# Strassen steps in more of a decoder layer's products

## The chip, the core and the metric

The kernel runs on one core of one Trainium2 chip. The metric is device time of one execution in microseconds (us), as the median of several runs. TensorE (PE) multiplies, VectorE (DVE) and ScalarE (ACT) do elementwise work, GpSimd (POOL) little here, SyncE (SP) issues the loads of the weights.

## The reference, cut to what matters

One layer of a decoder for 256 tokens with a model width of 2048, all in float32.

```
h  = RMSNorm(x);  z = h @ W_in          # W_in: 2048 x 19472
q, k, v, g, lr = first columns of z     # gated linear attention: 1024, 1024, 2048, 2048, 16
gk = log_sigmoid(lr @ w_gk_up + b_gk) / 16
A  = GLA(q, k, v, gk) * silu(g), normed # 4 heads, keys 256, values 512 wide
Bm = dilated attention on 9 x 1024 columns of z
y  = sigmoid(ga) * (A @ W_a) + sigmoid(gb) * (Bm @ W_b)
x  = x + y @ W_out                      # 2048 x 2048
x  = x + (silu(n @ W_gate) * (n @ W_up)) @ W_down,  n = RMSNorm(x)   # width 5632
out = RMSNorm(x)
```

## The kernel before, in words

Every product is a Job. Its weights stream in units of 1 MB at most through a ring of three raw tiles (dma). Each unit is cut into pieces of at most 1024 columns of float32 (subs). ACT rounds a piece to fp32r (wh), DVE subtracts to get the rest (wl), and TensorE forms a product as three matmuls: high by high, high by low, low by high. The activations are split the same way beforehand (HiLo).

Jobs have kinds. "T" holds the activations as stationary operand and moves the weights (512 columns in two PSUM banks); "F" holds the weights and moves 256 tokens; "G" is F with high and low activations in one matmul. "S" takes two column blocks of 512 at once in eight steps of 256 weight rows (add_steps, lines 161 to 190); a step listed in `fast` forms seven block products instead of eight, with sums of weight blocks made by DVE (sums, L187) and sums of activation blocks made beforehand (x1_forms, L886 to 900). An S job needs all eight PSUM banks: of p2, p3, p4, p8 and of p1, p5, p6, p7 one set lies in the four acc banks, the other in psa and psb, and `turn` says which (step_bank, L218).

The order is written out. The main loop goes through all pieces; for piece i it splits piece i + 4 (LA = 4; the wh and wl rings have five buffers each, and from the feed-forward S jobs on there is a sixth pair in z8 and z9), then, at the first piece of a job, evacuates the job before (pending.evac), runs a hook (pre), advances the queue of side work by one, issues the piece's matmuls, and advances the queue by one again. Side work are generators in a first-in first-out queue: attention heads, transposes (turn_block, ffn_norm_chunk), the forms. `drain` runs what is left of a tag at once. Each engine works through its own instructions in the order in which they were issued.

Only ten feed-forward jobs (fast_pair) are S jobs, each with three fast steps (2, 4, 6). The linear attention's values, gates, keys and queries, the output projection (w_out, four T jobs) and the down products (down: groups of 4, 4 and 3 blocks of 512 rows, four T jobs each) are plain. The 16 columns of the decay input lr ride behind the gates of heads 2 and 3: 1040 columns are cut into three T jobs of 348, 346 and 346 columns, which run first.

Of the kernel before, what the change touches and what calls it, by code (L numbers as in the profile page):

```python
# [23 lines left out]
NEG = -1e30  # L24

# [21 lines left out]
class Job:  # L47
# [14 lines left out]
    def __init__(self, kind, w, row0, nkt, col0, ncols, ktu, acts, evac, pre=None, pairs=None,  # L62
                 col1=None, fast=(), forms=None, turn=0):
        self.pairs = pairs
        self.col1, self.fast, self.forms = col1, fast, forms
        self.bank, self.turn = {}, turn
# [6 lines left out]
def trunk_layer(ctx: ExitStack, tc: tile.TileContext, x, attn_norm, w_in, w_gk_up, b_gk, gla_norm,  # L73
# [114 lines left out]
    def sums(sub):  # L188

        if sub.get("src") not in ("t13", "t24"):  # L190
            return
        b = raw_step(sub["unit"])
        if sub["src"] == "t13":
            t = sub["unit"]["t"] = env["fp"].tile([P, 4, 512], F32, name="t", tag="t")
            nc.vector.tensor_sub(t[:, 0:2], b[:, :, 1], b[:, 0])
        else:
            t = sub["unit"]["t"]
            nc.vector.tensor_sub(t[:, 2], b[:, 1, 1], t[:, 0])
            nc.vector.tensor_sub(t[:, 3], b[:, 1, 0], t[:, 2])  # L199

    def step_src(sub):
        b = raw_step(sub["unit"])
        src = sub["src"]
        if src == "b11":
            return b[:, 0, 0:1]
        if src[0] == "b":
            return b[:, int(src[1]) - 1]
        return sub["unit"]["t"][:, 0:2] if src == "t13" else sub["unit"]["t"][:, 2:4]
# [90 lines left out]
    def mains(sub, only=None, part=None):  # L299
# [6 lines left out]
        if not hasattr(job, "acc"):  # L306
# [6 lines left out]
            elif n <= 256:  # L313
                t = ps_acc()
                job.acc = [t[:, 0:256], t[:, 256:512]]
# [137 lines left out]
    def view(key, slot, a, fresh=True):  # L453

        if key not in env:
            env[key] = block("z", slot).rearrange("p (a t) -> p a t", a=a)
# [15 lines left out]
    def g_chunk(lo, hi, slots, base):  # L472

        def go(job):
            for a in range(2):
                c = lo
                while c < hi:
                    sc = env["rstd"][:, a:a + 1]
                    if c >= 1024:
                        act(lrn[:, a], job.acc[a][:, c - lo:hi - lo], AF.Copy, scale=sc)  # L480
                        c = hi
                        continue
                    j = c // 512
                    e = min(hi, (j + 1) * 512)
                    g = view(("g", base + j), slots[j], 2)
                    act(g[:, a, c - j * 512:e - j * 512], job.acc[a][:, c - lo:e - lo],
                                         AF.Silu, scale=sc)
                    c = e
        return go
# [10 lines left out]
    def evac_zf(key, slot):  # L500
        def go(job):
            scaled(job, view(key, slot, 4), "R")
        return go
# [11 lines left out]
    def gla_head(h, half):  # L515
# [94 lines left out]
        hl = hl_block("o", {2: 4, 3: 6, 0: 0, 1: 2}[h])  # L610
# [25 lines left out]
    def open_dil():  # L636
        drain("bias")
        drain("B")
# [94 lines left out]
    def win(kind, col, n, evac, pre=None):  # L733
        add(Job(kind, w_in, 0, KT, col, n, 8 if n <= 256 else 4, h_acts, evac, pre))

    def start_half(tag, heads):
        def go():
            for h in heads:
                push(tag, gla_head(h, tag))
        return go  # L740

    c0 = C_G + 1024
    for lo, hi in ((0, 348), (348, 694), (694, 1040)):
        ev = g_chunk(lo, hi, (0, 1), 2)
        if hi == 1040:
            def ev(job, f=ev):
                f(job)
                push("A", gla_lr())
        win("T", c0 + lo, hi - lo, ev)
    win("F", C_K + 512, 512, evac_zf(("k", "A"), 2))  # L750
    win("F", C_Q + 512, 512, evac_zf(("q", "A"), 3))
    win("T", C_V + 1024, 512, evac_t(("v", 2), 4))
    win("T", C_V + 1536, 512, evac_t(("v", 3), 5, start_half("A", (2, 3))))
    win("T", C_G, 512, g_chunk(0, 512, (6, 7), 0))
    win("T", C_G + 512, 512, g_chunk(512, 1024, (6, 7), 0))
    win("F", C_K, 512, evac_zf(("k", "B"), 8))
    win("F", C_Q, 512, evac_zf(("q", "B"), 9), {0: lambda: drain("A")})
    win("T", C_V, 512, evac_t(("v", 0), 0))

    def after_b():  # L760
        start_half("B", (0, 1))()
        push("bias", bias_table())
    win("T", C_V + 512, 512, evac_t(("v", 1), 1, after_b))


# [8 lines left out]
    for r in range(4):  # L774
        for g in range(3):
            base = C_DIL + 3072 * g + 256 * r
            first = {0: lambda r=r: drain(f"D{r - 2}")} if g == 0 else None
            slot = ((2, 3, 4), (8, 0, 1))[r % 2][g]
# [7 lines left out]
        if r % 2 == 0:  # L786

            for g in range(3):
                then = (first_heads if r == 0 else lambda: push_heads(2)) if g == 2 else None
                first = {0: lambda r=r: drain("D1" if r else "B")} if g == 1 else None  # L790
# [92 lines left out]
    FAST = (2, 4, 6)  # L883
    x1F = {}

    def x1_forms():  # L886

        yield from idle(1)
        for n, st in enumerate(FAST):
            t = x1T[st // 2].t[st % 2]  # L890
            a = env["fp"].tile([P, 2, S], F32, name="fa", tag="u0")
            f = env["fp"].tile([P, 4, P], F32, name="ff", tag="u1")
            nc.vector.tensor_add(a, t[:, :, 0].bitcast(F32), t[:, :, 1].bitcast(F32))
            nc.vector.tensor_add(f[:, 0], a[:, 0, P:], a[:, 1, P:])
            nc.vector.tensor_sub(f[:, 2], a[:, 0, 0:P], a[:, 0, P:])
            nc.vector.tensor_sub(f[:, 1], f[:, 0], a[:, 0, 0:P])
            nc.vector.tensor_sub(f[:, 3], a[:, 1, 0:P], f[:, 1])
            b = x1F[st] = block("o", n, F32R).rearrange("p (w f q) -> p w f q", w=2, f=4)
            act(b[:, 0], f, AF.Copy)
            nc.vector.tensor_sub(b[:, 1], f, b[:, 0].bitcast(F32))  # L900
            yield
            yield

    def ffn_norm_chunk(c):
# [5 lines left out]
        if c == 3:  # L910
# [3 lines left out]
            push("F", x1_forms())  # L914

    def evac_out(c):
        def go(job):
            for a in range(2):
                nc.vector.tensor_add(x1[c][:, a], job.acc[a], x1[c][:, a])
                junk = env["fp"].tile([P, 512], F32, name="junk", tag="u3")  # L920
                act(junk, x1[c][:, a], AF.Square, accum_out=ss1[:, a, c:c + 1])
# [18 lines left out]

    def turn_up(p, z, n, pair):
        aT[p] = hl_block("z", 2 * p % 8)
        push("A", turn_block(z, aT[p], n, pair))

# [9 lines left out]
    def evac_step1(job):  # L954

        u = job.u = [env["fp"].tile([P, 512], F32, name=f"u{i}", tag=f"u{i}") for i in range(4)]
        b = job.bank
        act(u[0], b["p1"], AF.Copy)
        nc.vector.tensor_add(u[1], u[0], b["p6"])
        nc.vector.tensor_add(u[2], u[1], b["p7"])  # L960
        nc.vector.tensor_add(u[1], u[1], b["p5"])
        nc.vector.tensor_add(u[3], u[2], b["p5"])

    def evac_step2(p):
        def go(job):
            u, b = job.u, job.bank
            z = env["fp"].tile([P, 2, 512], F32, name="sg", tag="sg", bufs=2)
            nc.vector.tensor_add(z[:, 0], u[0], b["p2"])
            act(z[:, 0], z[:, 0], AF.Silu, scale=env["rstd2"][:, 0:1])
            nc.vector.tensor_add(u[1], u[1], b["p3"])  # L970
            nc.vector.tensor_add(z[:, 1], u[2], b["p4"])
            act(z[:, 1], z[:, 1], AF.Silu, scale=env["rstd2"][:, 1:2])
            nc.vector.tensor_add(u[3], u[3], b["p8"])
            for a in range(2):
                nc.vector.scalar_tensor_tensor(z[:, a], u[1 + 2 * a], env["rstd2"][:, a:a + 1], z[:, a],
                                               op0=ALU.mult, op1=ALU.mult)
            turn_up(p, z, 2, 2 * job.turn)
        return go

    def evac_down(c, last):  # L980
        def go(job):
            for a in range(2):
                nc.vector.tensor_add(x1[c][:, a], job.acc[a], x1[c][:, a])
                if last:
                    junk = env["fp"].tile([P, 512], F32, name="junk", tag="u3")
# [13 lines left out]
    def fast_pair(p, turn):  # L999
        def start():  # L1000
            drain("F")
            drain("A")
        job = Job("S", w_ffn_in, 0, KT, 512 * p, 512, 2, x1_acts, evac_step2(p), {4: start}, None,
                  FF + 512 * p, FAST, lambda st: x1F[st], turn)
        add(job)
        job.pre[len(job.subs) - 2] = lambda: evac_step1(job)

    def down(p0, n, last):
        acts = lambda ki, p0=p0: (aT[p0 + ki // 4], ki % 4)
        for c in range(4):  # L1010
            pre = {2 * (n - 1): lambda: drain("A")} if c == 0 else None
            if c == 0 and last:
                pre[0] = load_fg
            add(Job("T", w_ffn_out, p0 * 512, 4 * n, 512 * c, 512, 4, acts, evac_down(c, last), pre,
                    pairs=[((3, 0, 1, 3), (0, 1, 0, 3))[p0 == 4][c]]))

    pair(0)
    for p in range(1, 11):
        fast_pair(p, (0, 0, 1, 0, 0, 1, 0, 1, 0, 1, 0)[p])
# [13 lines left out]
    more = next(i for i, s in enumerate(subs) if s["job"].kind == "S") + LA + 1  # L1033
# [47 lines left out]
    def input_rstd():  # L1081
# [5 lines left out]
        env["R"] = row_bcast("R", env["rstd"])  # L1087

# [38 lines left out]
    def add_tokens(src, a, q):  # L1127
        w = slice(q * S, q * S + S)
        nc.vector.tensor_add(x1[3][:, a, w], src, x1[3][:, a, w])
        junk = env["fp"].tile([P, 512], F32, name="junk", tag="u3")  # L1130
# [74 lines left out]
```

## Time and profile before

| | us |
|---|---|
| median of 3 runs (1863.65 to 1865.05) | 1864.06 |
| the profiled execution | 1863.59 |
| its span, first to last instruction | 1861.5 |
| TensorE busy in the span | 1847.5 |
| VectorE busy | 1197.6 |
| ScalarE busy | 913.2 |

The profile is one execution. The page gives busy time by engine, 40 slices of the span and groups of instructions; the chain of waits follows the work that ended last, backwards from the end. The timeline shows instructions in order with the time that the engine stood idle before them and what released it. Matmuls are pipelined: the length shown for one contains its way through the array, so the distance between starts is what one costs.

### The profile page before, as it was taken

The numbers are of one execution on the slowest core, as the hardware profiler recorded it, in microseconds if no ns is written. First come the engines' busy times: TensorE is split into PE (matmuls) and PEld (weight loads), VectorE is DVE, ScalarE is ACT, GpSimd is POOL, SyncE is SP. The second block draws the span as 40 slices with busy tenths as digits, with TensorE's granted clock in tenths as the row PEclk, the third lists the DMA queues.
The fourth block names the chain that finished last, engine by engine and source line by source line (L and its number), as shares of the span: only waits on it lengthen the run. The fifth ranks groups of instructions, "written<-read, shape, count | busy, mean of one in ns | idle before, by whom it ended". The sixth has DMA issues, their size and how long they took to land.

```text
span 1861.5 us, 23268 instructions
## 1 busy us (share of the span) xinstructions
PE 1847.5 (99%) x9234; PEld 1572.2 (84%) x9234; DVE 1197.6 (64%) x1394; ACT 913.2 (49%) x1144; POOL 22.3 (1%) x35
## 2 busy tenths in 40 slices
PE   8999999999999999999999999999999999999998
PEld 8988988888888888888888888888888888888887
DVE  6446646745665466655545556789647998559974
ACT  6446545544444444544444455555435555335553
POOL 0000000000000000000000000000000000000001
PEclk9999999999999999999999999999999999999999
DMA  7554455455555566466656655555655655545562
GB/s 253 205 195 167 159 187 176 162 182 186 179 176 181 192 182 209 147 199 207 205 201 218 234 182 180 192 193 204 219 188 189 217 183 205 201 161 203 202 236 103
DMA packets 208580, 356.33 MB, mean 191 GB/s; under 512 B 7403, under 2 KB 67879, under 8 KB 208472
## 3 DMA queue, kind: packets, MB, share of 16 engines
q1 hardware_dynamic: 203472, 346.19, 54.1%
q0 software_dynamic: 1728, 5.51, 1.4%
q10 hardware_dynamic: 3272, 3.16, 0.6%
q8 instruction: 72, 1.18, 0.2%
q14 instruction: 36, 0.29, 0.0%
HBM read 352.70 MB, written 2.13 MB: 191 GB/s over the span
## 4 chain that ended last, share of the span: by engine, by line
PE 99%; DMA 0%; DVE 0%; ACT 0%; SPq 0%; issue 0%; DVEq 0%; ACTq 0%
PE acc L356 51%; PE acc L236 12%; PE acc L332 10%; PE psb L356 6%; PE psa L236 5%; PE acc L335 5%; PE psb L236 5%; PE psa L672 1%; PE psb L717 0%; PE psa L593 0%; PE psa L818 0%; PE psb L575 0%; PE psb L682 0%; PE psb L719 0%; PE acc L818 0%; PE psa L693 0%
## 5 line engine op out<-in xcount | busy, mean ns | idle before, releaser
L133 ACT ACTIVATE wh<-raw 128x1024 fp32r<-128x1024 f32 (+3 forms) x614 | 625.8, 1026 | 633.6 <-PE acc L356 435.6
L296 DVE TENSOR_TENSOR wl<-raw,wh 128x1024 fp32r<-128x1024 f32 (+2 forms) x482 | 580.9, 1212 | 505.7 <-ACT wh L133 503.8
L356 PE MATMUL acc<-wh,h 128*128 128x512 f32 (+2 forms) x1536 | 469.8, 383 | 0.0
L356 PEld LDWEIGHTS acc<-wh,h 128*128 128x128 f32 x1536 | 286.6, 188 | 54.2 <-issue 1.3
L356 PE MATMUL acc<-wl,h 128*128 128x512 f32 (+2 forms) x768 | 292.9, 381 | 0.0
L332 PE MATMUL acc<-h,wh 128*128 128x512 f32 x768 | 196.4, 397 | 0.0
L356 PE MATMUL acc<-wh,z 128*128 128x512 f32 x600 | 187.8, 390 | 0.0
L289 DVE TENSOR_TENSOR wl<-raw,wh 128x1024 fp32r<-128x1024 f32 (+1 forms) x132 | 143.1, 1100 | 42.3 <-ACT wh L133 41.9
L356 PEld LDWEIGHTS acc<-wl,h 128*128 128x128 f32 x768 | 144.7, 188 | 25.5
L332 PEld LDWEIGHTS acc<-h,wh 128*128 128x128 f32 x768 | 138.5, 189 | 26.9 <-issue 0.7
L236 PE MATMUL acc<-wh,h 128*128 128x512 f32 x446 | 146.7, 390 | 0.0
L356 PEld LDWEIGHTS acc<-wh,z 128*128 128x128 f32 x600 | 112.6, 188 | 23.2
L356 PE MATMUL acc<-wl,z 128*128 128x512 f32 x300 | 116.7, 389 | 0.0
L335 PEld LDWEIGHTS acc<-h,wl 128*128 128x128 f32 x768 | 104.6, 190 | 7.8
L335 PE MATMUL acc<-h,wl 128*128 128x256 f32 x768 | 106.9, 282 | 0.0
L236 PEld LDWEIGHTS acc<-wh,h 128*128 128x128 f32 x446 | 83.7, 188 | 17.3
L356 PE MATMUL acc<-h,wh 128*128 128x256 f32 x512 | 92.5, 283 | 0.0
L236 PE MATMUL acc<-wl,h 128*128 128x512 f32 x223 | 86.8, 389 | 0.0
L133 ACT ACTIVATE wh<-t 128x1024 fp32r<-128x1024 f32 x51 | 54.1, 1060 | 58.4 <-DVE t L199 26.5
L356 PEld LDWEIGHTS acc<-h,wh 128*128 128x128 f32 x512 | 80.0, 192 | 0.2
L356 PE MATMUL acc<-wh,o 128*128 128x512 f32 x256 | 79.4, 389 | 0.0
L356 PE MATMUL psb<-wh,z 128*128 128x512 f32 (+1 forms) x248 | 75.8, 381 | 0.0
(276 smaller groups left out, 2308.6 us busy)
## 6 DMA issues: line engine op xcount, KB each, us to landing
raw<-in_w_in_dram SPq DMA_DIRECT2D x144, 1024.0 KB, 4.7
raw<-in_w_ffn_in_dram SPq DMA_DIRECT2D x160, 512.0 KB, 4.4
raw<-in_w_ffn_out_dram SPq DMA_DIRECT2D x44, 1024.0 KB, 5.0
raw<-in_w_branch_gla_dram SPq DMA_DIRECT2D x16, 1024.0 KB, 5.0
raw<-in_w_out_dram SPq DMA_DIRECT2D x16, 1024.0 KB, 4.9
raw<-in_w_branch_dil_dram SPq DMA_DIRECT2D x8, 1024.0 KB, 4.9
raw<-in_w_ffn_in_dram SPq DMA_DIRECT2D x8, 1024.0 KB, 4.7
raw<-in_w_in_dram SPq DMA_DIRECT2D x8, 692.0 KB, 4.0
```

The costliest lines, as they stand in the source:

```text
L133: nc.scalar.activation(o, i, func, **kw)
L236: nc.tensor.matmul(job.bank[pr["b"]], st, mv, start=pr["first"] and i == 0, stop=pr["last"] and i == 2, skip_group_check=True)
L289: nc.vector.tensor_sub(wl, src, wh.bitcast(F32))
L296: nc.vector.tensor_sub(wl[:, :k * n], src, wh[:, :k * n].bitcast(F32))
L332: nc.tensor.matmul(job.acc[j], wh[:, kk, c], hl.both(aj), start=ki == 0, stop=ki == job.nkt - 1, skip_group_check=True)
L335: nc.tensor.matmul(job.acc[j][:, 0:S], wl[:, kk, c], hl.hi(aj), start=False, stop=ki == job.nkt - 1, skip_group_check=True)
L356: nc.tensor.matmul(dst, st, mv, start=first and i == 0 and j % per_bank == 0, stop=last and i == 2, skip_group_check=True)
L672: nc.tensor.matmul(p1[:, g * 256:(g + 1) * 256], qk[g][:, 0, 128:256], qk[g][:, 1], start=g != 1, stop=True, skip_group_check=True)
```

## The change: what it does

The S job is put into one function (fast_job) with its two evacuations, and used in more places. The forms of the activations (act_forms) are made for the normed input, for the merged heads, and for parts of the feed-forward activations.

- Gates and values of the linear attention: four S jobs with three fast steps each, on heads (2, 3) and (0, 1). The keys and queries of heads 2 and 3 come first, then lr as a T job of its own with 16 columns, in one unit of 16 blocks of 128 rows, then the four S jobs, then keys and queries of heads 0 and 1. Heads 2 and 3 are pushed behind the last S job.
- Output projection: chunk 0 as a T job, chunks 1 and 2 as one S job with three fast steps, chunk 3 as a T job in the psb banks.
- Down product: in the first two groups two S jobs with two fast steps (2, 5) each; the third stays.
- The sums of weight blocks have two tiles (t13, t24) instead of one. The `turn` of the feed-forward jobs follows a new list, and the banks of the last down jobs as well.

```diff
+    def act_forms(blocks, out, dst, tmp, steps=FAST):
+        yield from idle(1)
+        for n, st in enumerate(steps):
+            t = blocks[st // 2].t[st % 2]
+            a, f = tmp(0).rearrange("p (a q) -> p a q", a=2), tmp(1).rearrange("p (f q) -> p f q", f=4)
+            nc.vector.tensor_add(a, t[:, :, 0].bitcast(F32), t[:, :, 1].bitcast(F32))
+            nc.vector.tensor_add(f[:, 0], a[:, 0, P:], a[:, 1, P:])
...
+            act(b[:, 0], f, AF.Copy)
+            nc.vector.tensor_sub(b[:, 1], f, b[:, 0].bitcast(F32))
+            yield
+            yield
+
+    def fast_job(w, col0, col1, acts, forms, turn, tile, dst, evac, pre, row0=0, fast=FAST, plus=None):
+        def first(job):
+            c = job.c = dst()
+            b = job.bank
+            act(c[0], b["p1"], AF.Copy)
+            nc.vector.tensor_add(c[1], c[0], b["p6"])
+            nc.vector.tensor_add(c[2], c[1], b["p7"])
+            nc.vector.tensor_add(c[1], c[1], b["p5"])
+            nc.vector.tensor_add(c[3], c[2], b["p5"])
+            if plus:
+                job.u, job.c = c, plus()
+                for u, c in zip(job.u, job.c):
+                    nc.vector.tensor_add(c, c, u)
+        def second(job):
+            for i, n in ((0, "p2"), (2, "p4"), (1, "p3"), (3, "p8")):
+                nc.vector.tensor_add(job.c[i], job.c[i], job.bank[n])
+                evac(job, i)
+        job = Job("S", w, row0, KT, col0, 512, 2, acts, second, pre, None, col1, fast, lambda st: forms[st], turn, tile)
+        add(job)
+        job.pre[next(i for i, s in enumerate(job.subs) if s["step"] > max(fast))] = lambda: first(job)
...
+    def evac_lr(job):
+        for a in range(2):
+            act(lrn[:, a], job.acc[a], AF.Copy, scale=env["rstd"][:, a:a + 1])
+        push("L", gla_lr())
...
-    for lo, hi in ((0, 348), (348, 694), (694, 1040)):
...
-        win("T", c0 + lo, hi - lo, ev)
...
-    win("T", C_V + 512, 512, evac_t(("v", 1), 1, after_b))
+    win("F", C_K + 512, 512, evac_zf(("k", "A"), 6))
+    win("F", C_Q + 512, 512, evac_zf(("q", "A"), 7))
+    win("T", C_LR, 16, evac_lr)
+    win_fast("g", (2, 3), (3, 5), C_G + 1024, 0, AF.Silu, {4: first_fast})
+    win_fast("g", (0, 1), (8, 9), C_G, 1, AF.Silu, {})
+    win_fast("v", (2, 3), (2, 4), C_V + 1024, 0, AF.Copy, {})
+    win_fast("v", (0, 1), (0, 1), C_V, 1, AF.Copy, {}, last_values)
+    win("F", C_K, 512, evac_zf(("k", "B"), ("o", 0)))
+    win("F", C_Q, 512, evac_zf(("q", "B"), ("o", 1), after_b))
...
-    for c in range(4):
-        add(Job("T", w_out, 0, KT, 512 * c, 512, 4, merged_acts, evac_out(c),
-                {0: reload_x} if c == 0 else None))
+    def out_forms():
+        reload_x()
+        push("mF", act_forms(merged, mF, lambda n: fp_forms(n) if n < 2 else block("o", 2, F32R),
+                             lambda i: block("o", i)[:, 0:512]))
...
+    add(Job("T", w_out, 0, KT, 0, 512, 4, merged_acts, evac_out(0), {0: out_forms}))
+    fast_job(w_out, 512, 1024, merged_acts, mF, 0, fp_tile, four_halves, evac_out2, {4: out_start},
+             plus=lambda: four_x1(1))
+    add(Job("T", w_out, 0, KT, 1536, 512, 4, merged_acts, evac_out(3), pairs=[3]))
...
     def turn_up(p, z, n, pair):
         aT[p] = hl_block("z", 2 * p % 8)
         push("A", turn_block(z, aT[p], n, pair))
+        if p in (1, 2, 5, 6):
+            st, f = ((2, 0), (5, 1))[p % 4 - 1]
+            push("A", act_forms([None] * (st // 2) + [aT[p]], aF, lambda n: fp_forms(f),
+                                lambda i: fp_half(f"u{i}"), (st,)))
...
     def down(p0, n, last):
+        if not last:
+            for c in (0, 2):
+                turn = int(c == 0)
+                pre = {4: lambda: drain("A")} if c == 0 else {}
+                fast_job(w_ffn_out, 512 * c, 512 * c + 512, acts, aF, turn, fp_tile, four_halves,
+                         lambda job, i: None, pre, p0 * 512, (2, 5), lambda c=c: four_x1(c))
+            return
```

## Rows read from the trace of the kernel before

**Rows 1.** The page: busy time of each engine, and VectorE's tenths in 40 slices.

```profile
PE 1847.5 (99%) x9234; PEld 1572.2 (84%) x9234; DVE 1197.6 (64%) x1394; ACT 913.2 (49%) x1144; POOL 22.3 (1%) x35
...
DVE  6446646745665466655545556789647998559974
```

**Rows 2.** The chain of waits in order of time: start us, length us, what.

```profile
1166.70 21.76 PE psb L356 x96
...
1848.60 4.33 PE psa L356 x36
```

**Rows 3.** Two stretches: length; busy us of PE, PEld, DVE, ACT, POOL; clock, DMA share, GB/s.

```profile
33.00:57.00 24.00, 24.00 (x153) 24.00 (x153) 12.47 (x13) 14.00 (x21) 0.00 (x0) 1.00 0.67 226
...
1244.00:1286.40 42.40, 42.40 (x192) 35.17 (x191) 38.80 (x44) 24.23 (x28) 0.00 (x0) 1.00 0.58 198
```

**Rows 4.** Timeline of TensorE, 1238 to 1282: start us, length us, engine, line.

```profile
1238.84 1.03 PE L818 MATMUL acc<-ident,sg 128*128 128x128 f32 x8
...
1273.05 0.39 PE L236 MATMUL acc<-wh,h 128*128 128x512 f32 x1
...
1281.21 1.03 PE L818 MATMUL psa<-ident,sg 128*128 128x128 f32 x8
```

**Rows 5.** Timeline of TensorE and its weight loads (PEld), 162 to 165.

```profile
162.48 1.06 PE L575 MATMUL psb<-qe,ke 128*128 128x128 f32 x8
...
163.38 0.61 PE L575 MATMUL psb<-mA,sA 128*128 128x128 f32 x4
...
163.91 0.54 PEld L575 LDWEIGHTS psb<-qe,kd 128*64 128x64 f32 x8
...
164.52 0.19 PEld L356 LDWEIGHTS acc<-wh,h 128*128 128x128 f32 x1
...
164.63 0.19 PEld L356 LDWEIGHTS acc<-wl,h 128*128 128x128 f32 x1
```

**Rows 6.** Stretches at the program's start and end, columns as in rows 3.

```profile
4.00:8.00 4.00, 2.38 (x10) 1.78 (x10) 1.84 (x4) 1.55 (x4) 0.00 (x0) 1.00 1.03 340
...
1850.00:1853.00 3.00, 2.92 (x25) 2.71 (x23) 0.04 (x1) 0.00 (x0) 0.00 (x0) 1.00 0.52 193
...
1856.00:1857.00 1.00, 0.00 (x0) 0.00 (x0) 0.99 (x2) 0.23 (x1) 0.00 (x0) 0.77 0.19 76
```

**Rows 7.** Groups of instructions by shape: busy us, mean ns, idle before.

```profile
L133 ACT ACTIVATE wh<-raw 128x1024 fp32r<-128x1024 f32 x560 | 589.7, 1058 | 611.1 <-PE acc L356 429.0 <-PE acc L332 71.8 <-PE psb L356 36.3
...
L296 DVE TENSOR_TENSOR wl<-raw,wh 128x1024 fp32r<-128x1024 f32 x458 | 560.1, 1229 | 495.1 <-ACT wh L133 493.3
```

**Rows 8.** Timeline of all engines, 0 to 40.

```profile
6.11 0.78 ACT L133 ACTIVATE wh<-raw 128x696 fp32r<-128x696 f32 x1
...
7.05 0.87 DVE L296 TENSOR_TENSOR wl<-raw,wh 128x696 fp32r<-128x696 f32 x1
...
8.01 0.63 PE L356 MATMUL acc<-wl,h 128*128 128x348 f32 x1
...
8.43 0.79 PE L356 MATMUL acc<-wh,h 128*128 128x348 f32 x2
...
10.07 0.47 PE L356 MATMUL acc<-wh,h 128*128 128x348 f32 x2
```

**Rows 9.** Timeline of VectorE, 1155 to 1192.

```profile
1156.96 1.23 DVE L296 TENSOR_TENSOR wl<-raw,wh 128x1024 fp32r<-128x1024 f32 x1 [0.26 <-ACT wh L133]
...
1161.49 1.23 DVE L296 TENSOR_TENSOR wl<-raw,wh 128x1024 fp32r<-128x1024 f32 x1 [0.26 <-ACT wh L133]
...
1166.03 1.23 DVE L296 TENSOR_TENSOR wl<-raw,wh 128x1024 fp32r<-128x1024 f32 x1 [0.26 <-ACT wh L133]
...
1170.56 2.36 DVE L296 TENSOR_TENSOR wl<-raw,wh 128x1024 fp32r<-128x1024 f32 x2 [0.26 <-ACT wh L133]
```

**Rows 10.** Timeline of VectorE, 1262 to 1279.

```profile
1270.05 0.68 DVE L959 TENSOR_TENSOR u<-u,acc 128x512 f32<-128x512 f32 x1
...
1272.09 0.68 DVE L962 TENSOR_TENSOR u<-u,acc 128x512 f32<-128x512 f32 x1
```

More of the change, by code (lines that the diff above doesn't have):

```diff
@@ L62, in __init__ @@
     def __init__(self, kind, w, row0, nkt, col0, ncols, ktu, acts, evac, pre=None, pairs=None,
-                 col1=None, fast=(), forms=None, turn=0):
+                 col1=None, fast=(), forms=None, turn=0, tile=None):
         self.pairs = pairs
         self.col1, self.fast, self.forms = col1, fast, forms
-        self.bank, self.turn = {}, turn
+        self.bank, self.turn, self.tile = {}, turn, tile
         self.kind, self.w, self.row0, self.nkt = kind, w, row0, nkt
@@ L314, in mains @@
                 t = ps_acc()
-                job.acc = [t[:, 0:256], t[:, 256:512]]
+                job.acc = [t[:, 0:n], t[:, 256:256 + n]]
                 job.banks = [t]
@@ new lines, in start_half, with win_fast, dst, evac @@
+    def start_half(half, heads):
+        for h in heads:
+            push(f"{half}{h}", gla_head(h, half))
+    hF = {}
+    def win_fast(name, heads, slots, col, turn, func, pre, then=None):
+        def dst():
+            v = [view((name, h), slot, 2) for h, slot in zip(heads, slots)]
+            return [v[i % 2][:, i // 2] for i in range(4)]
+        def evac(job, i):
+            act(job.c[i], job.c[i], func, scale=env["rstd"][:, i // 2:i // 2 + 1])
+            if then and i == 3:
+                then()
+        fast_job(w_in, col, col + 512, h_acts, hF, turn, lambda t: block("o", int(t == "t24")), dst, evac, pre)
@@ L766, in push_heads, with drain_b @@
+    win_fast("g", (0, 1), (8, 9), C_G, 1, AF.Silu, {})
[3 more added lines that the diff above has]
+    win("F", C_Q, 512, evac_zf(("q", "B"), ("o", 1), after_b))
+    def drain_b():
+        for t in ("B0", "B1", "bias"):
+            drain(t)
     def push_heads(r):
@@ L952, in evac_fup @@
         return go
[L954 to L978, printed above, removed]
     def evac_down(c, last):
@@ L1002, in start, with dst, evac @@
             drain("A")
[L1003 to L1006, printed above, removed]
+        def dst():
+            z = env["sg"] = env["fp"].tile([P, 2, 512], F32, name="sg", tag="sg", bufs=2)
+            return z[:, 0], fp_half("u0"), z[:, 1], fp_half("u1")
+        def evac(job, i):
+            a = i // 2
+            r = env["rstd2"][:, a:a + 1]
+            if i % 2 == 0:
+                act(job.c[i], job.c[i], AF.Silu, scale=r)
+                return
+            nc.vector.scalar_tensor_tensor(job.c[2 * a], job.c[i], r, job.c[2 * a], op0=ALU.mult, op1=ALU.mult)
+            if a:
+                turn_up(p, env["sg"], 2, 2 * turn)
+        fast_job(w_ffn_in, 512 * p, FF + 512 * p, x1_acts, x1F, turn, fp_tile, dst, evac, {4: start})
     def down(p0, n, last):
         acts = lambda ki, p0=p0: (aT[p0 + ki // 4], ki % 4)
+        if not last:
[4 more added lines that the diff above has]
+                         lambda job, i: None, pre, p0 * 512, (2, 5), lambda c=c: four_x1(c))
+            return
         for c in range(4):
[L1011 to L1013 removed]
+            pre = {2 * (n - 1): lambda: drain("A"), 0: load_fg} if c == 0 else None
             add(Job("T", w_ffn_out, p0 * 512, 4 * n, 512 * c, 512, 4, acts, evac_down(c, last), pre,
[L1015 removed]
+                    pairs=[(0, 1, 3, 0)[c]]))
     pair(0)
     for p in range(1, 11):
[L1019 removed]
+        fast_pair(p, (0, 0, 1, 0, 1, 0, 1, 0, 1, 0, 1)[p])
         if p in (3, 7):
@@ L1032, in trunk_layer @@
     state = dict(unit=0, split=0)
-    more = next(i for i, s in enumerate(subs) if s["job"].kind == "S") + LA + 1
+    more = next(i for i, s in enumerate(subs) if s["job"].w is w_ffn_in and s["job"].kind == "S") + LA + 1
     for i, s in enumerate(subs):
```

129 lines of the change are left out of this document (56 added, 73 removed).

## The prediction

> **What bounds the kernel now.** I read the page first: TensorE is busy 99% of the span and carries the whole chain of waits; VectorE is busy 64% on average, but its row of slices reaches 9 tenths in the last third, where the feed-forward products already take Strassen steps [rows 1]. So time is the sum of matmul spacings plus whatever makes TensorE wait. The chain in order of time gives the spacings at full clock: 96 matmuls of 512 columns in 21.76 us, 0.2267 us each; 36 of 256 columns in 4.33 us, 0.120 each [rows 2]. The stretches give 24.0 us for about 152 matmuls of 346 columns, 0.158 each [rows 3]; 348 columns I take at 0.159. A step (two blocks of 128 weight rows times 1024 columns, 256 tokens) takes 24 matmuls plain and 21 as a Strassen step. That this arrives on TensorE is seen between two equal transposes of two consecutive fast jobs: 1281.21 - 1238.84 = 42.37 us [rows 4], which is 183 x 0.2267 = 41.49 plus eight transposes, 0.88. VectorE is at 38.8 of 42.4 us there [rows 3], and TensorE still does not wait.
>
> **The change, part by part.** The sum is made against the profiled execution, 1863.59 us (span 1861.5); the median of the runs shown, 1864.06, is 0.47 above it, which I add at the end.
>
> Strassen steps: four jobs of three steps (gates and values), one of three (output projection), four of two (down products), 23 steps. Each saves three matmuls: 69 x 0.2267 = -15.64 us.
>
> The 1040 columns of gates and decay input were three jobs of 348, 346 and 346 columns: 96 x 0.159 + 192 x 0.158 = 45.60 us. The 1024 gate columns at 512 are 192 x 0.2267 = 43.53 before the Strassen saving already counted: -2.07 us.
>
> The 16 decay columns become a job of their own: 16 blocks x 2 token halves x 3 = 96 matmuls of 16 columns, each with its own 128 x 128 weight load. No row has such a matmul. What it cannot go below is the weight load: where two loads follow each other at once, they start at 164.52 and 164.63, 0.108 us apart in the unrounded times; eight matmuls of 128 columns start over 163.38 - 162.48 = 0.90 us, 0.112 each [rows 5]. From above, it is no dearer than the 0.120 of 256 columns. I take 0.112, the nearest row: +10.75 us (10.4 to 11.5). So nearly all that gates and values gain goes back here. The Trainium skill (TensorE: Matmul & The Clock Gate, section Back-to-back issue gap) gives the smallest matmuls a floor near 25 ns; by that, an estimate, the decay job would take 2.4 us and the sum would be 8.4 us lower. The weight loads of this trace stand against it [rows 5].
>
> Start: the first job now takes 512 columns instead of 348, so the first weight unit is 168 KB larger. At 340 GB/s [rows 6] that is 0.49 us. Its split is 1024 columns instead of 696: ACT 1.06 us for 0.78, VectorE 1.23 for 0.87 [rows 7, 8]. Before, the second matmul waits for wl and starts at 8.01 [rows 8]; now the third does, near 9.1. One matmul more is done by then, and part of the loss falls into the time at low clock (the pair at 8.43 against the pair at 10.07 [rows 8]). +0.8 us (0.3 to 1.5).
>
> Output projection. Here I expect a wait that the trace shows only in its parts. The first chunk (plain) uses two of the four acc banks. The fast job after it has turn 0 and needs all four in its first step: p4 and p8 get the banks of that first chunk, and p4 starts after six matmuls, 1.36 us into the job. Those banks are freed by two adds on VectorE (evac_out), queued behind the weight splits and behind the three act_forms steps of mF, which run at the fifth, sixth and seventh of the chunk's eight pieces. The same offsets exist before, in the first feed-forward gate job: splits there start at 1156.96, 1161.49, 1166.03, so each piece with a form takes 4.53 us where TensorE needs 2.72, and two more splits start at 1170.56 [rows 9] while TensorE began the next job at 1166.70 [rows 2]. It cost nothing there, because the next job took psb banks. In the new place the second of these two splits is half size (0.6), so the first add starts about 1172.3 - 1166.7 = 5.6 us into the fast job and ends 0.7 later [rows 10]. TensorE waits 6.3 - 1.4 = +4.9 us. If VectorE were not late, the add would end near 2.1 us: lower bound 0.8; upper 5.8.
>
> Clock behind that wait: at the end of the program the last matmul lies in 1850 to 1853 and the granted clock falls in 1856 to 1857 [rows 6], 3 to 4 us later, sooner than 4.9. At the start the engine did seven matmuls at half speed before it rose [rows 8], worth 1.2 us. I take +1.2 (0 to 2.5).
>
> Heads: the first matmul of head 2 (psb) comes one piece, 24 x 0.120 = 2.9 us, into the K job behind the last values job, whose p4 bank it takes over. VectorE reaches that bank's add after a split (ACT 1.06 and VectorE 1.23 from the end of the job [rows 7], with 0.1 before each) and one other add, and ends it some 3.75 us after the job (adds 0.6 apart, 0.68 long [rows 10]). +0.85 us, and ACT's four copies there can delay the head's next steps by 0 to 1.35: +0.25. Together +1.1 (0.9 to 2.2). The heads' 21 queue steps each, twice two heads and 10 of the bias table are 94 of 96 slots before they are drained, so nothing is forced.
>
> Down products: the aF forms (3.4 us of VectorE each, 4.53 less a split, 1.14 [rows 9]) enter four of the fast jobs. VectorE has 3.6 us to spare in 42.4 [rows 3], and the add that frees p5 ends at 1272.77, 0.96 us before p3 of the next job needs its bank (1273.05 plus three matmuls [rows 4, 10]). +0.4 us for two such places (0 to 2). Attention's fast jobs, with one ring pair fewer than the feed-forward ones, have no turn_block and no closing multiplications, so some 36 of 41.5 us on VectorE, and pieces ready 2 us or more ahead: 0. The decay job's weights are 131 KB; 10.75 us of TensorE time cover them: 0. The forms of hT run during the Q job, and the decay job covers their lag: 0.
>
> Sum: -15.64 - 2.07 + 10.75 + 0.8 + 4.9 + 1.2 + 1.1 + 0.4 = +1.44 us; 1863.59 + 1.44 + 0.47 = **1865.5 us**, no change that can be measured. This case alone: 1861.5 to 1869.
>
> **The rivals.**
> (1) The clock falls inside the decay job (slower). For 10.75 us the array is given 16 columns per weight load; nothing in the trace before is that thin for so long. The few transposes before 7.6 us left the engine at half speed too: 0.79 us for the pair of matmuls at 8.43, 0.47 for the same pair at 10.07 [rows 8]. If the chip takes the decay job for rest, the clock falls in it as it does behind the last matmul [rows 6], there 3 to 4 us later; the 64 loads then left take twice 0.108 us: +6.9, and the first fast job starts slow, +1.2. 1865.5 + 8.1 = 1873.6; it decides against the change from about 3 us of this on. Against it: the weight loader is never idle there. The Trainium skill (same page, section Part 1: The HAM clock gate) says that the clock follows how busy the array has been and is halved when it rests; whether weight loads count it does not say, and no run here shows it.
> (2) No late add at the output projection (faster): if the forms cost VectorE less than in rows 9, the wait is 0.8 and no clock is lost: -5.3, 1860.2.
> (3) The decay matmuls run like the smallest of the trace, 64 columns with 64-column loads, eight in 0.54 us or 0.058 apart [rows 5]: 96 x 0.054 = 5.2 less, 1860.3. Against it: those loads are half as wide.
> (4) VectorE becomes the bound in attention's fast jobs: with one ring pair fewer, each of 12 fast steps waits, say, 0.7 us, half a piece: +8.4, 1873.9. For it: a fast step has 5.5 operations of 1024 columns on VectorE, 6.8 us at 1.23 [rows 7], for TensorE's 4.8; against it, the plain step between gives 5.44 - 2.46 = 3.0 back.
>
> **How the numbers follow.** Chances: forecast 0.42, rival 1 0.38, rival 2 0.08, rival 3 0.04, rival 4 0.08. 0.2% is 3.7 us, about what a measurement of this kernel can tell from no change: bounds 1860.3 and 1867.8. Faster: half of rivals 2 and 3, and 0.05 of the forecast's lower end: 0.11. Slower: rivals 1 and 4 almost whole, and 0.05 of the forecast's upper end: 0.49. Within: 0.40. Range over the cases, 8 in 10: 1858.5 to 1875.
>
> **What would show it.** The decay job as 96 matmuls 0.11 us apart (right), 0.22 in its later part or 0.06 and less (rivals 1, 3). A gap of some 5 us on TensorE about 1.4 us into the output projection's fast job, ended by the add of line evac_out. First matmuls of head 2 waiting under 1 us on a VectorE add into psb. Fast jobs without transposes of 41.5 us; longer ones with waits on wl would be rival 4. The prediction is wrong if the output projection shows no wait, or if the clock leaves its upper level for long.

## The result and the profile after

| | before | after |
|---|---|---|
| median of the runs, us | 1864.22 (1863.65 to 1865.05) | 1875.97 (1874.99 to 1876.51) |
| the profiled execution | 1863.59 | 1875.82 |
| its span | 1861.5 | 1874.0 |
| TensorE busy | 1847.5 | 1852.4 |
| VectorE busy | 1197.6 | 1354.4 |

The changed kernel is slower: 1.0062 times the time before, 95% interval 1.0045 to 1.008. I had forecast 1865.5 us, no change, in a range up to 1875.0. The time is 10.5 us above the forecast and 1.0 above the range. What happened is rival 1, the clock that falls in the decay job, and three small terms more.

The page of the changed kernel answers to [rows 1]; TensorE's clock in the last line is in tenths of full speed:

```profile
PE 1852.4 (99%) x9165; PEld 1570.3 (84%) x9165; DVE 1354.4 (72%) x1634; ACT 950.6 (51%) x1194; POOL 22.1 (1%) x35
...
DVE  6588877755666466655555577789978999889874
...
PEclk9899999999999999999999999999999999999999
```

TensorE issues 69 matmuls fewer and yet is busy 4.9 us longer, so waits alone can't be the reason. VectorE works 157 us more, and the second slice of the clock shows an 8, where the page of the kernel before shows 9 throughout.

**The decay job.** Four stretches of the changed kernel, columns as in [rows 3]: the job's first 4.5 us, its rest, the first matmuls of the gates' job behind it, and as long again after these.

```profile
59.70:64.20 4.50, 4.50 (x44) 4.50 (x42) 3.48 (x8) 2.53 (x3) 0.00 (x0) 1.00 0.67 237
64.30:75.80 11.50, 11.50 (x56) 11.50 (x56) 1.92 (x3) 0.00 (x0) 0.00 (x0) 0.50 0.26 91
75.90:81.10 5.20, 5.20 (x13) 3.73 (x14) 1.83 (x2) 0.96 (x3) 0.00 (x0) 0.50 0.00 0
81.40:86.60 5.20, 5.20 (x25) 4.33 (x24) 3.60 (x4) 2.38 (x3) 0.00 (x0) 1.00 0.08 17
```

The timeline of TensorE where the first stretch ends (start us, length us, engine, line, operation):

```profile
63.84 0.37 PE L398 MATMUL acc<-wh,h 128*128 128x16 f32 x2
64.06 0.26 PE L398 MATMUL acc<-wl,h 128*128 128x16 f32 x1
64.17 0.54 PE L398 MATMUL acc<-wh,h 128*128 128x16 f32 x2
64.56 0.36 PE L398 MATMUL acc<-wl,h 128*128 128x16 f32 x1
64.77 0.36 PE L398 MATMUL acc<-wh,h 128*128 128x16 f32 x1
```

Three matmuls take 63.84 to 64.17, 0.11 us each, as forecast; from about 64.2 on they stand 0.21 apart. The job lasts from 59.67 to 75.87, 16.2 us instead of 10.75. Its granted clock is 1.00 (2.4 GHz) in the first stretch and 0.50 (1.2 GHz) in the second, although the column of weight loads shows the loader busy for all of it. The gates' job begins at 0.50 too: twelve spacings of 512 columns, from 75.87 to 81.13, take 5.26 us for 12 x 0.2267 = 2.72. In the other four profiled runs with this job the fall came 3.8 to 4.6 us into it; each time its slow loads and the slow matmuls behind it cost 8.0 to 8.1 us together.

**The output projection.** The timeline of TensorE at p4's wait, and a stretch behind it:

```profile
1087.72 0.39 PE L278 MATMUL acc<-wh,z 128*128 128x512 f32 x1
1093.07 0.79 PE L278 MATMUL acc<-wh,z 128*128 128x512 f32 x1 [4.96 <-DVE o L950]
...
1093.10:1098.40 5.30, 5.30 (x13) 4.14 (x14) 2.92 (x4) 2.46 (x5) 0.00 (x0) 0.50 0.52 194
```

VectorE on the way to that add, answering to [rows 9]:

```profile
1077.01 1.23 DVE L331 TENSOR_TENSOR wl<-raw,wh 128x1024 fp32r<-128x1024 f32 x1 [1.49 <-ACT wh L134]
...
1081.53 1.22 DVE L331 TENSOR_TENSOR wl<-raw,wh 128x1024 fp32r<-128x1024 f32 x1 [0.26 <-ACT wh L134]
...
1086.07 1.22 DVE L331 TENSOR_TENSOR wl<-raw,wh 128x1024 fp32r<-128x1024 f32 x1 [0.26 <-ACT wh L134]
...
1090.59 1.83 DVE L331 TENSOR_TENSOR wl<-raw,wh 128x1024 fp32r<-128x1024 f32 x2 [0.26 <-ACT wh L134]
1092.34 1.28 DVE L950 TENSOR_TENSOR o<-acc,o 128x512 f32<-128x512 f32 x2
```

The splits come 4.53 us apart, a form between each two, and the adds that free p4's bank only after the last of them. TensorE waits 4.96 us, and the clock is at 0.50 behind the wait: twelve spacings from 1093.07 to 1098.36 take 5.29 us for 2.72.

All waits of TensorE between 40 us and the end (what waits, for what, us in total, times, longest):

```profile
PE acc L278 <- DVE o L950: 5.0, 1, 5.0
PE psa L465 <- issue: 1.1, 1, 1.1
PE psb L550 <- DVE z L246: 0.7, 1, 0.7
```

The third is head 2, forecast at 0.85. The second, at 1149.94, I hadn't forecast: the transposes of x1's chunk 2, behind those of chunk 1 on the same psa bank. The profile names no releaser for it ("issue"), but VectorE's last read of that bank ends at 1149.84, 0.1 us before.

**Ledger**, us against the profiled execution before:

| term | forecast | measured |
|---|---|---|
| 69 matmuls of 512 columns | -15.64 | -15.64 (spacing unchanged) |
| repacking of 1040 columns | -2.07 | -2.07 (spacing unchanged) |
| decay job | +10.75 | +16.20 |
| slow start of the gates' job, and two transposes (0.22 for 0.14 before) | 0 | +2.54 +0.08 |
| start of the program | +0.8 | +1.44 |
| p4's wait | +4.9 | +4.96 |
| clock behind it | +1.2 | +2.57 |
| heads | +1.1 | +0.74 |
| down product | +0.4 | 0 |
| transposes of x1's chunk 2 | not seen | +1.08 |
| sum | +1.44 | +11.90 (profiles: 12.23) |

The start's 1.44 comes from where the first two jobs of 192 matmuls end: 59.67 - 384 x 0.120 = 13.59, before 57.75 - 45.60 = 12.15. The clock has a part in it too:

```profile
8.24 0.78 PE L398 MATMUL acc<-h,wh 128*128 128x256 f32 x2
...
12.65 0.41 PE L398 MATMUL acc<-h,wl 128*128 128x256 f32 x1
12.87 0.48 PE L398 MATMUL acc<-h,wh 128*128 128x256 f32 x2
13.18 0.28 PE L398 MATMUL acc<-h,wl 128*128 128x256 f32 x1
```

The first matmul starts 0.67 us later than before (8.24 for 7.57), and some 22 of 256 columns stand 0.21 us apart before they go over to 0.12 near 13.0, which costs about 2 us; before, some seven matmuls of 348 columns ran at half speed, for about 1. In the other profiled runs that keep the first weight units, it was 16 to 23 matmuls.

### The profile page after: what moved, and what is told of

Read it like the earlier page. It is cut to its first block, busy times and chain, and to the rows that moved or that the text cites. A ratio compares the mean times of both kernels' runs of the same rounds, so it can differ in the third digit from the quotient of the medians.

```text
span 1874.0 us, 23611 instructions
## 1 busy us (share of the span) xinstructions
PE 1852.4 (99%) x9165; PEld 1570.3 (84%) x9165; DVE 1354.4 (72%) x1634; ACT 950.6 (51%) x1194; POOL 22.1 (1%) x35
## 4 chain that ended last, share of the span: by engine, by line
PE 98%; DVE 1%; DMA 1%; ACT 0%; issue 0%; SPq 0%; DVEq 0%; ACTq 0%
PE acc L398 33%; PE acc L278 22%; PE psa L278 11%; PE psb L278 10%; PE acc L374 9%; PE acc L377 5%; PE psb L398 3%; PE psa L700 1%; PE psa L863 0%; PE psb L745 0%; PE psa L623 0%; PE psb L605 0%; DMA o<-in_x_dram 0%; PE psb L710 0%; ACT wh L134 0%; PE psb L747 0%
## 5 line engine op out<-in xcount | busy, mean ns | idle before, releaser
L134 ACT ACTIVATE wh<-raw 128x1024 fp32r<-128x1024 f32 (+1 forms) x610 | 613.8, 1019 | 516.2 <-PE acc L398 249.7
L338 DVE TENSOR_TENSOR wl<-raw,wh 128x1024 fp32r<-128x1024 f32 x341 | 415.4, 1226 | 321.7 <-ACT wh L134 319.3
L331 DVE TENSOR_TENSOR wl<-raw,wh 128x1024 fp32r<-128x1024 f32 (+1 forms) x269 | 292.1, 1115 | 80.4 <-ACT wh L134 79.6
L398 PE MATMUL acc<-wh,h 128*128 128x512 f32 (+1 forms) x1024 | 317.0, 387 | 0.0
L398 PEld LDWEIGHTS acc<-wh,h 128*128 128x128 f32 x1024 | 194.5, 193 | 39.0 <-issue 1.9
L398 PE MATMUL acc<-wl,h 128*128 128x512 f32 (+1 forms) x512 | 196.9, 385 | 0.0
L278 PEld LDWEIGHTS acc<-wh,h 128*128 128x128 f32 x588 | 111.5, 190 | 23.5 <-ACT lrn L134 0.3
L134 ACT ACTIVATE wh<-t 128x1024 fp32r<-128x1024 f32 x67 | 71.0, 1060 | 91.7 <-DVE t L199 32.1
L278 PE MATMUL psb<-wh,h 128*128 128x512 f32 x328 | 117.2, 389 | 0.0
L278 PE MATMUL psa<-wh,h 128*128 128x512 f32 x286 | 101.1, 390 | 0.0
L278 PE MATMUL acc<-wh,z 128*128 128x512 f32 x270 | 89.1, 397 | 5.0 <-DVE o L950 5.0
L331 DVE TENSOR_TENSOR wl<-t,wh 128x1024 fp32r<-128x1024 f32 x67 | 81.8, 1221 | 6.4 <-ACT wh L134 4.7
```

What stands on the lines that cost most here:

```text
L134: nc.scalar.activation(o, i, func, **kw)
L278: nc.tensor.matmul(job.bank[pr["b"]], st, mv, start=pr["first"] and i == 0, stop=pr["last"] and i == 2, skip_group_check=True)
L331: nc.vector.tensor_sub(wl, src, wh.bitcast(F32))
L338: nc.vector.tensor_sub(wl[:, :k * n], src, wh[:, :k * n].bitcast(F32))
L398: nc.tensor.matmul(dst, st, mv, start=first and i == 0 and j % per_bank == 0, stop=last and i == 2, skip_group_check=True)
```

## The experiments

Theory: the Strassen saving arrives whole; the clock (at the decay job and behind p4's wait), the load-bound decay job and p4's wait eat it. The main rival: VectorE, 72% busy now, is the bound, and what is taken from TensorE comes back as waits. Edits are to the changed kernel; ratios are to the kernel before.

**Tokens move past the decay weights.**

```diff
+        if job.kind == "L":
+            job.acc = ps_acc()
+            for kk in range(sub["k"]):
+                hl, aj = job.acts(kk)
+                nc.tensor.matmul(job.acc[0:n], wh[:, kk], hl.both(aj), ...)
+                nc.tensor.matmul(job.acc[0:n, 0:S], wl[:, kk], hl.hi(aj), ...)
+            return
...
-    win("T", C_LR, 16, evac_lr)
+    win("L", C_LR, 16, evac_lr)
```

> The decay job computed the other way round: the 16 weight columns are the stationary operand, the tokens move (16 matmuls of 512 columns and 16 of 256 instead of 96 of 16). Theory 1 (thin matmuls: first bound by the weight load, then at half clock): the job takes 16 x (0.2267 + 0.120) = 5.55 us instead of 16.2, the clock stays at its upper level through it, the first fast job's twelve slow matmuls go (-2.54), two transposes go (-0.2): -13.4 us, 1862.6, and up to 2 us less of that if the forms of hT, which the longer job covered, are now late. Rival (VectorE's higher load is what costs): the shorter job uncovers VectorE, waits appear in the fast jobs behind it, and the time stays above 1870. A second rival (the clock falls because few columns of the array are used, whatever moves): spacing 0.45 in part of the job and a slow start of the fast job: about 1868.

Measured: 1861.72 us, 14.3 less than the changed kernel (13.65 between the profiled executions, for 13.4 expected); ratio 0.9985 (0.9975 to 0.9995). The decay job and as long a stretch of the gates' job behind it:

```profile
59.60:65.00 5.40, 5.40 (x33) 2.87 (x32) 4.38 (x9) 2.53 (x3) 0.00 (x0) 1.00 0.58 194
65.20:70.40 5.20, 5.20 (x25) 4.19 (x24) 4.51 (x8) 1.96 (x3) 0.00 (x0) 1.00 0.61 205
```

The 32 matmuls take 5.59 us (59.52 to 65.11), the clock stays at 1.00, and nothing waits behind them. VectorE's work is the same (1354.8 us), so VectorE was not the bound here. The second rival falls too: 16 of the array's columns hold weights, and the clock stays.

**The same matmuls, spread.** The 96 matmuls stay, twelve behind each piece of the Q job, in the free psa bank.

```diff
...
+        if sub["job"] is lr:
+            continue
         mains(sub)
+        if sub["job"] is jobs[2]:
+            lr_part(sub["idx"])
```

> The same 96 matmuls of 16 columns for the decay input, but issued twelve at a time behind each of the eight pieces of the Q job. Theory 1 (two costs, the weight load at 0.1115 us each and the clock that falls in a stretch of nothing else): the load cost stays, 96 x 0.1115 = 10.7 us, and the clock does not fall: -5.5 in the matmuls and -2.5 in the first fast job: -8.0 us, 1868.0. Rival (the clock falls from the mean load of the array, so the thin matmuls cost it wherever they stand): slow stretches inside the Q job, 1876 or more. If the thin matmuls were cheap among wide ones (the load hidden beside the wide matmul before it), up to 10 us more would go: 1858 to 1868.

Measured: 1866.77 us, 9.2 less; ratio 1.0014 (1.0005 to 1.0023). The whole stretch, and one group of twelve in it with the next wide matmul:

```profile
39.10:70.00 30.90, 30.90 (x268) 30.90 (x267) 18.92 (x34) 12.62 (x16) 0.00 (x0) 1.00 0.51 167
...
47.78 0.17 PE L354 MATMUL psa<-lrwh,h 128*128 128x16 f32 x1
47.81 0.26 PE L354 MATMUL psa<-lrwl,h 128*128 128x16 f32 x1
...
49.04 0.36 PE L414 MATMUL acc<-h,wh 128*128 128x256 f32 x1
```

Twelve take 49.04 - 47.78 = 1.26 us, 0.105 each: the first only 0.03, its load hidden beside the wide matmul ahead of it, the other eleven 0.112. The load's price stays, the clock's goes. So the two are separate costs: some 10 us for the loads, 8.0 (5.5 and 2.5) for the clock. It came out 1.2 us below what I expected: the cheaper spacing gives 96 x 0.0065 = 0.6, and in the profiled execution five slow matmuls fewer behind p4's wait give 1.0.

**The same loads with 128 columns each.**

```diff
-            act(lrn[:, a], job.acc[a], AF.Copy, scale=env["rstd"][:, a:a + 1])
+            act(lrn[:, a], job.acc[a][:, 0:16], AF.Copy, scale=env["rstd"][:, a:a + 1])
...
-    win("T", C_LR, 16, evac_lr)
+    win("T", C_LR, 128, evac_lr)
```

> The decay job loads 128 weight columns instead of 16 (the 112 beside them are computed and left unread), so that the same 96 weight loads each have a matmul of 128 columns. Theory 1 in the form 'few columns per load let the clock fall': 0.112 us apart as the 128-column matmuls of rows 5, 10.75 us instead of 16.2, no fall, no slow start of the fast job: -8.0 us, 1868.0. The rival form ('a stretch paced by weight loads counts as rest, whatever moves'): the same fall as in the changed kernel, 0.213 apart in its later part, 1876.

Measured: 1867.12 us, 8.9 less; ratio 1.0014 (1.0005 to 1.0023). The decay job and the start of the gates' job:

```profile
59.30:69.80 10.50, 10.50 (x97) 10.50 (x96) 8.04 (x12) 3.60 (x4) 0.00 (x0) 1.00 0.38 131
69.90:75.10 5.20, 5.20 (x26) 4.16 (x26) 2.86 (x3) 2.27 (x5) 0.00 (x0) 1.00 0.45 180
```

With eight times the columns the job is shorter: 10.7 us (59.23 to 69.91) at clock 1.00. The loader is as busy as in the changed kernel, 10.50 of 10.50 us, so a busy loader alone doesn't hold the clock up; what differs between the two runs is how many columns move behind each load, 16 or 128. The Trainium skill (TensorE: Matmul & The Clock Gate, section Part 1: The HAM clock gate) says that the clock follows how busy the array has been. These two runs agree, and weight loads alone didn't hold it up here.

**Psb banks for the first output chunk.**

```diff
-    add(Job("T", w_out, 0, KT, 0, 512, 4, merged_acts, evac_out(0), {0: out_forms}))
+    add(Job("T", w_out, 0, KT, 0, 512, 4, merged_acts, evac_out(0), {0: out_forms}, pairs=[3]))
```

> The plain first chunk of the output projection accumulates in the two psb banks instead of two acc banks. Theory 1 (p4 of the fast job waits for the late add, and the clock falls in that wait): the idle time of 4.96 us and the slow stretch of 2.6 us behind it both go: -7.6 us, 1868.4. Rival A (VectorE stays late and the next consumer of it waits instead: p1 in psb, two steps on): the wait moves by about 10 us and shrinks to under 1, the time falls by 6.6 to 7.6 all the same. Rival B (the clock falls there for another reason than the wait): -5.0 only, 1871.0, with the slow stretch still in the granted clock.

Measured: 1869.88 us, 6.1 less; ratio 1.003 (1.0018 to 1.0042). Timelines of the late adds and of TensorE, and a stretch around them:

```profile
1092.06 1.28 DVE L950 TENSOR_TENSOR o<-psb,o 128x512 f32<-128x512 f32 x2
...
1092.85 0.30 PE L465 MATMUL psa<-ident,o 128*128 128x128 f32 x1 [0.93 <-PE acc L278]
1093.40 0.98 PE L465 MATMUL psa<-ident,o 128*128 128x128 f32 x7 [0.26 <-DVE o L950]
...
1085.00:1100.00 15.00, 13.81 (x65) 11.13 (x64) 12.91 (x20) 8.82 (x16) 0.00 (x0) 1.00 0.44 137
```

p4's wait and the slow stretch are gone, the clock is 1.00 throughout. The adds are as late as before (1092.06 for 1092.34), and now their next reader waits for them, the transposes of x1's chunk 0: 0.93 + 0.26. The first of the two is put down to TensorE, whose matmul ahead began at 1091.53; the first of the two adds ends at 1092.74, 0.1 us before the transpose, so it is the adds' too. -4.96 - 2.57 + 1.19 = -6.3. So it is rival A's shape, at another reader and sooner than it said: VectorE's lateness stays, and costs 1.2 us at this reader instead of 7.5 at the other.

**One form instead of three.**

```diff
-        push("mF", act_forms(merged, mF, lambda n: fp_forms(n) if n < 2 else block("o", 2, F32R),
-                             lambda i: block("o", i)[:, 0:512]))
+        push("mF", act_forms(merged, mF, fp_forms, lambda i: block("o", i)[:, 0:512], (2,)))
...
         drain("mF")
+        mF[4] = mF[6] = mF[2]
```

> The output projection's forms mF are made for its first Strassen step only, and the other two steps use the same tile, so their products are computed from the wrong activations; TensorE's work is the same. Theory 1 (the add that frees p4's bank is late because VectorE is behind by three forms): with one form VectorE has caught up by the end of the first chunk, the wait falls from 4.96 to 0.8 to 1.5 us, the clock does not fall: -6 to -6.8 us, 1869.2 to 1870. Rival (the add is late for another reason, a full ring or the splits): the wait stays above 3 us and the time within 2 us of 1876.

Measured: 1869.3 us, 6.7 less; ratio 1.0027 (1.0016 to 1.0037). VectorE's adds and TensorE's waits between 1060 and 1155:

```profile
1088.06 1.28 DVE L950 TENSOR_TENSOR o<-acc,o 128x512 f32<-128x512 f32 x2
...
PE psa L465 <- issue: 1.1, 1, 1.1
PE acc L278 <- DVE o L950: 0.7, 1, 0.7
```

The adds begin 4.3 us sooner, the wait falls to 0.74, and the clock doesn't leave 1.00 after it. That settles what made the add late: the forms ahead of it in VectorE's queue.

**The output projection's Strassen job undone.**

```diff
...
-    fast_job(w_out, 512, 1024, merged_acts, mF, 0, fp_tile, four_halves, evac_out2, {4: out_start},
-             plus=lambda: four_x1(1))
+    for c in (1, 2):
+        add(Job("T", w_out, 0, KT, 512 * c, 512, 4, merged_acts, evac_out(c)))
```

> The output projection's two chunks back to plain ones (one Strassen job of three steps and its forms undone); decay job, gates, values and down product as in the changed kernel. By the trace this part saves 9 x 0.2267 = 2.04 us of matmuls and costs 4.96 of wait, 2.6 of slow clock and 1.08 at the transposes of x1's chunk 2: 6.6 us more than it saves, so without it 1876.0 - 6.6 = 1869.4. Rival (its gain reaches the end and the waits are ones that VectorE's backlog makes anywhere): 1874 or more, with the waits elsewhere.

Measured: 1868.67 us, 7.3 less; ratio 1.0022 (1.0013 to 1.0031). TensorE waits nowhere between 1060 and 1155, not at chunk 2's transposes either. This part of the change by itself saves 2 us of matmuls and costs over four times that (4.96 + 2.57 + 1.08 by the trace).

**The down product's Strassen steps undone.**

```diff
-            for c in (0, 2):
...
-                fast_job(w_ffn_out, 512 * c, 512 * c + 512, acts, aF, turn, fp_tile, four_halves,
-                         lambda job, i: None, pre, p0 * 512, (2, 5), lambda c=c: four_x1(c))
+            for c in range(4):
+                pre = {6: lambda: drain("A")} if c == 0 else None
+                add(Job("T", w_ffn_out, p0 * 512, 4 * n, 512 * c, 512, 4, acts, evac_down(c, last), pre,
+                        pairs=[(3, 0, 3, 1)[c]]))
```

> The two down products back to plain chunks (the eight Strassen steps undone, their forms still made on VectorE). If the steps' saving reaches the end whole (8 x 3 x 0.2267 = 5.44 us, and under 0.5 of waits in the fast jobs): +5.4 to +4.9, 1881.1. Rival (VectorE, busiest in this third of the program, already gives part of it back): +2 to +4, 1878 to 1880.

Measured: 1880.72 us, 4.8 more; ratio 1.0089 (1.0075 to 1.0103). That lies between the two expectations, but the median also carries what the start and the clock do from run to run: in the profiled execution p4's first matmul came 0.46 us sooner than in the changed kernel, and fewer matmuls behind its wait were slow. So I read the steps' saving between equal transposes ahead of and behind each of the two down products, here first and then in the changed kernel:

```profile
1340.61 1.03 PE L863 MATMUL acc<-ident,sg 128*128 128x128 f32 x8
1470.02 1.03 PE L863 MATMUL psa<-ident,sg 128*128 128x128 f32 x8
...
1341.46 1.03 PE L863 MATMUL acc<-ident,sg 128*128 128x128 f32 x8
1468.15 1.03 PE L863 MATMUL psa<-ident,sg 128*128 128x128 f32 x8
```

1470.02 - 1340.61 = 129.41 us, in the changed kernel 1468.15 - 1341.46 = 126.69: 2.72 us. The second product gives 2.73 (1597.14 to 1726.56 against 1595.27 to 1721.96). So 5.45 us for eight steps, against 5.44 by the spacing. The saving arrives whole where VectorE is busiest, and the rival with VectorE as the bound falls here as well.

**All mends together.** The wide decay job and psb banks, and PE work moved that the traces had shown waiting.

```diff
...
+        push("A2", idle(0))
         start_half("A", (2, 3))
...
     def ffn_norm_chunk(c):
-        yield from idle(1)
+        yield from idle({0: 2, 2: 3}.get(c, 1))
```

> The wide decay job and the psb banks for the first output chunk together, with queued PE work moved by one or two half-pieces where the traces showed it waiting: head 2's first matmul (0.74 us), the transposes of x1's chunk 0 (1.19 us in the run with psb banks) and of chunk 2 (1.07 us). If the costs add: 1861.7 - 6.1 - 0.74 - 1.19 - 1.07 = 1852.6. If the two share a cause (VectorE's total), the second brings less: 1855 to 1860.

Measured: 1853.99 us (1853.26 to 1854.51), ratio 0.9945 (0.9932 to 0.9957): 22.0 us below the changed kernel and 10.5 below the kernel before. All waits of TensorE in the program:

```profile
PE psb L1099 <- DMA grow<-in_attn_norm_dram: 3.8, 1, 3.8
PE psb L474 <- DVE h L464: 1.9, 1, 1.9
PE psa L278 <- DVE h L464: 1.3, 1, 1.3
```

The first two lie in the first 8 us, ahead of the first weights' matmuls, and are in the changed kernel as well (3.8 and 2.2). The 1.4 us by which the expected 1852.6 was missed is the last line, 1.27 us unrounded: x1's transposes, moved later, still hold psa when p7 wants it. The head's wait and chunk 2's are gone. Two more runs went on from here.

> As the kernel with all of these, and the first two weight units one block each instead of two, so that the first matmuls need 256 KB less ahead of them. If the wider first unit is what the start costs: -0.7 to -1.4 us against it, 1851.2 to 1851.9. Rival: the start waits for x's blocks and its transposes, and smaller units only add transfers: -0.3 to +0.5, 1852.3 to 1853.1.

```diff
-            u0, k = u1, 2 if not jobs[1:] and u1 < 4 else min(job.ktu, job.nkt - u1)
+            u0, k = u1, (1 if u1 < 2 else 2) if not jobs[1:] and u1 < 4 else min(job.ktu, job.nkt - u1)
```

Measured: 1853.98 us, ratio 0.9945 (0.9931 to 0.9958), the same. The first matmul comes 0.8 us sooner (7.16 for 7.96), and waits for wl of 0.59 and 0.23 us follow at 13.63 and 17.43, as much as was gained. In the profiled execution the decay job nevertheless starts 0.6 us sooner (59.04 for 59.65), with ten matmuls at half speed at the start instead of 23. The medians show no gain, and why not stays open.

> The wide decay job, psb banks for the first output chunk and head 2's first matmul one piece later, as before; and the transposes of x1's chunk 0 taken out of the Strassen job to the chunk behind it, so that neither they nor p7's psa bank wait there. The wait of 1.27 us at p7 in the run with all moves goes: 1854.0 - 1.3 = 1852.7. Rival: the three transposes of x1, now in one chunk on the same psa bank, wait for each other's readers, 1 us or more each, and the time is 1854 or above.

```diff
...
-            push("X", ffn_norm_chunk(c))
+            if c:
+                push("X", ffn_norm_chunk(c))
...
-            for c in (1, 2):
+            for c in (0, 1, 2):
```

Measured: 1854.4 us, ratio 0.9943 (0.9929 to 0.9956), the same again. p7's wait is gone and one of 1.39 us stands at a later transpose into psa: the rival, one wait of it.

```profile
1144.07 1.66 DVE L464 SCALAR_TENSOR_TENSOR h<-psa,cols,h 128x256 fp32r<-128x256 f32 x4 [2.40 <-ACT h L134]
...
1145.84 1.06 PE L474 MATMUL psa<-ident,o 128*128 128x128 f32 x8 [1.39 <-issue]
```

The profile names no releaser, but VectorE's reads of that bank end at 1145.73, 0.1 us before; and VectorE itself had stood idle for 2.40 us there, waiting for what ScalarE makes of the same bank (h). So this wait isn't a backlog of VectorE's: ScalarE came late to the bank, behind two squares that had waited 1.89 us for VectorE's last adds. In three orders of this work 1.2 to 1.4 us were lost at whichever reader came first; I have found no place where it costs nothing.

## Why the prediction was wrong

**The step that failed is the decay job's term: +10.75, with the clock at its upper level throughout and nothing for the job behind it.** Measured were 16.20 and 2.54 more behind it. The weight load's spacing in it held (0.11 us up to 64.2); what I had put at nothing was the clock's fall, which I named only as rival 1, with a chance of 0.38. Against it I had put that "the weight loader is never idle there". That was true and proved nothing: the loader was never idle, and the clock fell all the same. The evidence that spoke for the rival, that nothing in the trace is that thin for so long, was the better one, and the rows for it were there: transposes that left the engine at half speed [rows 8].

**Rival 1's mechanism was right, and its price right in sum, in part by luck.** It put 64 loads at twice the time and 1.2 us on the next job, 8.1 together. Measured: some 54 slow loads, 5.5 us, and 2.5 on the next job, 8.0: one part was 1.4 too high, the other 1.3 too low.

**The clock behind p4's wait was the term mis-sized**: 1.2 forecast, 2.57 measured. I had taken it from the start of the program, where some seven matmuls ran at half speed [rows 8]. Behind a wait it was 12 spacings in the changed kernel, and 7 (1.6 us) and 14 (3.0) in the runs with the spread job and with 128 columns, behind the same wait. It is a cost with a spread, and its upper end of 2.5 was too low. The Trainium skill (TensorE: Matmul & The Clock Gate, section Part 1: The HAM clock gate) warns that the number of matmuls at the lower level at a kernel's start differs from run to run of one kernel. These profiles, one execution of each kernel, show such a spread between kernels, at the start (16 to 23 matmuls) and behind the wait; none shows it within one kernel.

**The range missed by 1.0 us** because its upper end, 1875.0, was rival 1's sum and little more. Rival 1 keeps every other uncertain term: with the upper ends of p4's wait, the clock behind it and the start it reaches above 1876, and at a chance of 0.38 that belonged in the range. What came on top were the clock (+1.4 over the forecast), chunk 2's transposes (+1.1, not seen) and the start (+0.6, with more slow matmuls than before; in other runs the decay job started at 59.13 to 60.02, so this term was 0.9 to 1.8).

**What held.** The wait at p4: place, cause and size (4.9 and 4.96), with [rows 9] as its measure, and the run with one form shows the cause. Head 2: 0.85 and 0.74. The down product's forms: no wait in it. The saving of the steps: 5.45 for 5.44 where it was undone in the down products. Rival 4, VectorE as the bound in attention's fast jobs: no wait there, 34.1 us of VectorE work in 41.5 (81.40 to 122.90). Rival 2 (no late add) fell with p4's wait. Rival 3 (a spacing of 0.058) fell with 0.11 and 0.105.

## What to carry to other kernels

Before a narrow remainder is split off a wide product, price it twice: by the weight load for each matmul, and by what a long run of thin matmuls does to the clock; making the narrow operand stationary and moving the wide one avoided both here, 16.2 us to 5.6. A reader whose wait VectorE's backlog sets is best looked for by bank: who takes over this bank next, and how late is its last reader. A wait of several us costs more than itself where the clock falls in it; here, cutting one from 4.96 to 0.74 us kept the clock up and gave back more than the wait's length (6.7 us for 4.2).

## What the runs showed of the hardware

- A weight load of 128 x 128 takes its 0.11 us at the upper clock and 0.21 at the lower, so the lower clock doubles it as well.
- 96 loads with 16 columns each: the clock went to 0.50 at 64.2, 4.5 us into the job. The same 96 loads with 128 columns each, or twelve at a time between pieces of 256 columns: 1.00 throughout.
- Twelve thin matmuls between wide ones cost 0.03 us for the first and 0.112 for each that follows: the first one's load ran beside the wide matmul ahead of it (both start at 47.66), and the later ones paid theirs.
- A matmul with 16 stationary columns and 512 moving ones costs what a full one does: pairs of 512 and 256 columns stood 0.35 us apart, 0.2267 + 0.120.
